# Opening shared PSUM banks by the first product, storing pairs of tiles from two queues, and delaying the first squares in a decoder trunk

## The chip, the cores and the metric

The kernel runs on one core of a Trainium2 chip. The time is the device time of one execution in microseconds (us); before the change it is 1935.7 us, the median of three runs (1936.59, 1935.7, 1930.64). The engines are called as in the profile: PE (TensorE) with PEld for its weight loads, DVE (VectorE), ACT (ScalarE), POOL (GpSimd) and SP (SyncE, which here only issues DMAs).

## The reference, cut to what matters

A trunk of two layers works on 512 tokens and 16 meta tokens with a model width of 1024. Each layer is FFN, mixer, FFN; each of these has an RMS norm in front and one behind it, and is added to the residual stream `h`:

```python
def rmsnorm(x, g):
    return x * lax.rsqrt(jnp.mean(x * x, axis=-1, keepdims=True) + EPS) * g

def swiglu(x, w_in, w_out):
    gate, up = jnp.split(x @ w_in, 2, axis=-1)
    return (jax.nn.silu(gate) * up) @ w_out
```

Layer 0 mixes by chunked gated linear attention. Behind it one set of keys and values is made from `h`. Layer 1 mixes by sliding-window attention over that set. All is float32, the hidden width of the FFNs is 2816, and the 512 ordinary tokens of the last `h` are the output.

## The kernel before, in words

**Layout.** The residual stream `H` lies in SBUF as 128 partitions x 8 k tiles x 528 tokens, the features on the partitions. Layer 0 works on two groups of tokens, 272 and 256 (`L0`), layer 1 on two of 256 (`L1`). In the names of tiles, l0f is a first or second FFN of layer 0, l0m its mixer, kv the shared keys and values, l1f and l1m those of layer 1.

**A product** x @ w is made of three matmuls in fp32r (`mm3s`, L333): weight and operand are each split into a high and a low part, and high x high, low x high and high x low are added in one PSUM bank. The weights come by DMA as raw tiles of 128 x 512; `split_part` (L224) copies the high part on ACT (L226) and subtracts it on DVE (L227). The operand of an FFN or mixer is split in the same way by `Operand.build` (L425 on ACT, L426 on DVE).

**The norm** in front isn't applied to the operand but to the result, so the products needn't wait for it. `Operand.sumsq` squares the eight k tiles of `H`; squares 0 and 7 are kept (L399, ACT), 1 to 6 are squared on ACT (L402) and added on POOL (L403). `rstd` (L348) adds them over the partitions by products with ones (st_...), makes the reciprocal root in ten small operations on DVE or POOL (av, yv, zv, wv), puts it on a diagonal (dg, L383) and spreads it by a product (r_...). `Operand.factors` (L436) copies the result on ACT (R_..., L442). The gates need it: `gu` (L617), silu (L618), the up half (L621, L622) and the split of the hidden layer (`hid`, L407 and L408).

**The opening of an FFN or mixer** is `x_first` (L509): the first four units (128 output features each) of group 0, then of group 1, each over the eight k tiles, with the results kept in PSUM until the factor is there. A group of at most 256 tokens shares a bank between two units ("shared", L528): each has a half of 256 columns. As the products of the two units alternate, a product of 128 x 512 with a matrix of zeros opens each bank (L532, two per group), and the products add to it.

**The order of the work** is written out by a recorder, `Flow` (L60): jobs are generators with due times on a clock that each recorded product advances by its estimated time (L161 to L167). `flow.pump()`, called in `mm3s`, runs the jobs that are due. The order in which the jobs are run, with the waits that their data ask for, is the order in the queues of the engines. `spawn(job, delay)` sets when a job starts.

**The start of the kernel** (L1195 to L1244) loads the first k tiles of `H` and the first weights, builds group 0 (L1231 to L1235), spawns its squares, sum and factor (`factors(0)`, L1205, with a delay of 2.0; L1236) and group 1's operand (`second`, L1212, with a delay of 6.0; group 1's squares come when it is built). A square is due every 0.4 of the clock.

**The end** is `Residual.store` (L471): for each group and each pair of k tiles DVE multiplies the last FFN's result by its factor (L479), DVE or POOL (for the first two pairs of the last group) adds it to `H` (L480), and SP stores the two tiles, 128 KB each, by two DMAs (L482).

Of the kernel before, what the change touches and what calls it, by code (L numbers as in the profile page):

```python
# [16 lines left out]
P = 128  # L17
D = 1024
KD = 8
META = 16  # L20
# [103 lines left out]
def trunk_kernel(ctx: ExitStack, tc, a, out):  # L124
    nc = tc.nc
    pe, act, dve, pool, sp = nc.tensor, nc.scalar, nc.vector, nc.gpsimd, nc.sync
    flow = Flow()
# [7 lines left out]
    H = cp.tile([P, KD, TOK], F32, name="H")  # L135
# [6 lines left out]
    zeros = cp.tile([P, P], F32R, name="zeros")  # L142

    def ps(name):
        return pp.tile([P, 512], F32, tag="ps", name=name)

    def pair_tile(name, dt=F32R):
        return hp.tile([P, 2, TOK], dt, tag="pair", name=name)
# [5 lines left out]
    def flat(t):  # L154
        return t.rearrange("p a t -> p (a t)")

    def gain(layer, i, k):
        c = V_GAIN + layer * 48 + i * 8 + k
        return vec[:, c : c + 1]

    def mm(o, lhs, rhs, start=True, stop=True, onto=False):  # L161
        inst = pe.matmul(o, lhs, rhs, start=start, stop=stop, skip_group_check=onto)  # L162
        n = 1
        for d in rhs.shape[1:]:
            n *= d
        flow.clock += n / 2400 if rhs.dtype == F32R else max(n / 600, 0.12)
        return inst  # L167
# [41 lines left out]
    def set_ahead(n, slots=None):  # L209
        ahead[0], limit[0] = n, slots or n  # L210
        room[0].finish(flow)
        room[0] = Job(None)
# [11 lines left out]
    def split_part(i, raw, m):  # L224
        w = pair_tile(f"w{i}_{len(loaded[i])}")
        act.activation(w[:, 0, :m], raw[:, :m], AF.Copy)  # L226
        dve.tensor_tensor(w[:, 1, :m], raw[:, :m], w[:, 0, :m].bitcast(F32), op=ALU.subtract)  # L227
        loaded[i].append(w)
# [71 lines left out]
    def prefetch():  # L300
        while len(loaded) < cap[0] and asked[0] + costs[len(loaded)] <= freed[0] + ahead[0]:
            if isinstance(units[len(loaded)], list) and chains[0] == CHAINS:
                break
            load_unit()

    def next_w():
        used[0] += 1
        prefetch()
        flow.until(lambda: len(loaded) >= used[0])
        flow.wait(split_jobs[used[0] - 1])  # L310
        return loaded[used[0] - 1]
# [16 lines left out]
    def done_w(n=1):  # L328
        free_slots(sum(costs[released[0] : released[0] + n]))
        released[0] += n  # L330


    def mm3s(outs, j, x, g, start, stop, shared=False):  # L333
        t, n = g
        cols = slice(j % 4 * P, (j % 4 + 1) * P)
        xh, xl = x[:, 0, t : t + n], x[:, 1, t : t + n]
        for o, w in outs:
            mm(o, w[j // 4][:, 0, cols], xh, start and not shared, False)
            mm(o, w[j // 4][:, 1, cols], xh, False, False)
        for i, (o, w) in enumerate(outs):  # L340
            mm(o, w[j // 4][:, 0, cols], xl, False, stop and (not shared or i % 2 == 1))
            flow.pump()

    def mm3(o, w, j, x, g, start, stop):
        mm3s([(o, w)], j, x, g, start, stop)
# [64 lines left out]
    class Operand:  # L410
# [25 lines left out]
        def factors(self, gi, eng=pool):  # L436
            if self.rt is None:
                self.rt = sm.tile([P, TOK], F32, tag="R", name=f"R_{self.name}", bufs=2)
            o, n = self.groups[gi]
            yield FACT  # L440
            r = yield from rstd(self.accs[gi], n, D, False, f"{self.name}_{o}", eng)
            act.activation(self.rt[:, o : o + n], r[:, :n], AF.Copy)  # L442
# [5 lines left out]
    class Residual:  # L448
# [22 lines left out]
        def store(self, gi, g, r):  # L471
            o, n = g
            rb = r[:, :n].unsqueeze(1).to_broadcast([P, 2, n])
            for k in range(0, KD, 2):
                h, y = H[:, k : k + 2, o : o + n], Y[:, k : k + 2, o : o + n]
                last = gi == 1 and k < 4
                t = flat(pair_tile(f"t_{self.name}{k}", F32))[:, :512] if last else ps(f"t_{self.name}{gi}{k}")
                t = t.rearrange("p (k n) -> p k n", n=n)
                dve.tensor_tensor(t, y, rb, op=ALU.mult)  # L479
                (pool if last else dve).tensor_tensor(h, t, h, op=ALU.add)  # L480
                for j in (k, k + 1):
                    sp.dma_start(out[j, :, o - META : o - META + n], H[:, j, o : o + n])  # L482
                yield 1.0


# [23 lines left out]
    def x_first(x, nu, evac, opening=False, behind=(), first_ahead=8):  # L509
        behind = list(behind)  # L510
        ws = [] if opening else [next_w() for _ in range(nu)]
        set_ahead(8 if opening else 2 * first_ahead)
        jobs = []

        def drain(gi, g, some, pst):
            yield x.rjob[gi]
            for i, p in zip(some, pst):
                evac(i, g, p)
                yield 0.6

        both = range(nu)
        order = [(0, both[: nu // 2]), (0, both[nu // 2 :])] if opening else [(0, both)]
        for gi, some in order + [(1, both)]:
            g = x.groups[gi]
            n = g[1]
            while len(ws) <= some[-1]:
                ws.append(next_w())
            shared = n <= 256  # L528
            if shared:
                banks = [ps(f"x{used[0]}_{i}_{gi}") for i in some[::2]]  # L530
                for b in banks:
                    mm(b.rearrange("p (a c) -> p a c", c=P), zeros, zeros.unsqueeze(1).to_broadcast([P, 4, P]), True, False)  # L532
                pst = [banks[i // 2][:, i % 2 * 256 : i % 2 * 256 + n] for i in range(len(some))]
            else:
                pst = [ps(f"x{used[0]}_{i}_{gi}")[:, :n] for i in some]
            for k in range(KD):
                x.need(gi, k)
                mm3s([(p, ws[i]) for i, p in zip(some, pst)], k, x.tiles[k], g, k == 0, k == KD - 1, shared)
            flow.until(lambda: x.rjob[gi] is not None)
            jobs.append(flow.spawn(drain(gi, g, some, pst)))  # L540
            if gi == 0 and some[-1] == nu - 1:
                cap[0] = len(units)
                prefetch()
            if behind:
                flow.spawn(behind.pop(0))
        done_w(nu)
        return jobs
# [56 lines left out]
    def ffn(x, groups, finish, opening=False, tail=4):  # L604
# [31 lines left out]
        for ci, (lo, hi) in enumerate(FF_CHUNKS):  # L636
            hids = []
            if ci == 0:
                jobs = x_first(x, 4, evac_to([new_hid() for _ in range(2)]), opening)
                set_ahead(16, 4)  # L640
                factors = flow.spawn(right_factors(x, halves, z, plain))
                for t in range(2, hi):
                    jobs += x_units(x, 2, groups, evac_to([new_hid()]))
                plain.finish(flow)
                set_ahead(16, 8)
            else:
                flow.wait(factors)
                set_ahead(16, RING)
                tiles = Strassen(z, halves)
                cur = tiles.head(new_hid())  # L650
                while cur:
                    tiles.body(cur)
                    nxt = tiles.head(new_hid()) if len(hids) < hi - lo else None
                    jobs.append(tiles.tail(cur, nxt is None))
                    cur = nxt
            flow.wait(*jobs)
            if lo < LAST:
                out_proj(hids, groups, x.groups, ci == 0)
            else:
                set_ahead(32)  # L660
                cap[0] = min(used[0] + NLAST + tail, len(units))
                out_proj(hids, groups, x.groups, False, finish, KD, True)
# [119 lines left out]
    def gla(x, finish):  # L782
        set_ahead(10)
        with tc.tile_pool(name="gp", bufs=1) as gp:
# [193 lines left out]

            kinds = [("lr", 0), ("k", 0), ("q", 0), ("v", 0)]
            drained = x_first(x, 4, lambda i, g, p: evac(*kinds[i], g, p), first_ahead=5)  # L980
            flow.spawn(resets())
            gate = flow.spawn(gates(drained))
# [23 lines left out]
    def shared_kv(x, kp, behind):  # L1006
# [21 lines left out]
        def place(drained):  # L1028
# [3 lines left out]
            for j in range(2):  # L1032
# [21 lines left out]
                yield 1.0  # L1054

        job = flow.spawn(place(x_first(x, 4, evac, behind=behind, first_ahead=6)))
        return (kz, vt, vmz), job

# [139 lines left out]
    x = Operand("l0f0", lambda k: gain(0, 0, k), L0)  # L1198
# [32 lines left out]
    for c in (0, 512):  # L1231
        for k in range(c // 128, c // 128 + 4):
            x.build(0, k)
            if k % 4 < 2:
                split_part(k % 4, raws[k % 4][c // 512], 512)  # L1235
    x.rjob[0] = flow.spawn(factors(0), 2.0)  # L1236
    dma_end[0] = 1.0
    load_unit()
    load_unit()
# [13 lines left out]
    x = nxt  # L1253
    nxt, fin = into("l0f1", 0, 3, False, lambda k: gain(0, 4, k), L0)
    gla(x, fin)
    x = nxt
# [4 lines left out]
    with tc.tile_pool(name="kp", bufs=1) as kp:  # L1261
        x = Operand("l1f0", lambda k: gain(1, 0, k), L1)
# [10 lines left out]
        x = nxt  # L1273
# [88 lines left out]
```

## Time and profile before

| what | us |
|---|---|
| median of three runs | 1935.7 |
| the runs | 1936.59, 1935.7, 1930.64 |
| the profiled execution | 1931.38 |
| its span, first to last instruction | 1929.5 |
| PE busy | 1888.9 (98%) |
| DVE busy | 1420.1 (74%) |
| ACT busy | 1001.7 (52%) |
| POOL busy | 215.1 (11%) |
| mean granted clock of PE | 0.996 |

The profile is that of one execution, the one in the table. In a row of the timeline the columns are the start and the length in us, the engine, the line of the kernel, the operation, output <- inputs by the program's names (without their numbers), shapes and the count of the instructions joined; in brackets stands how long the engine was idle before, and what ended that. The lines are those of the kernel before; in the changed one they are higher by three from L333 on, and by one from L532 on. In a row of windows come the busy time of PE, PEld, DVE, ACT and POOL with their instructions, the granted clock, the share of the DMA engines and GB/s.

### The profile page before, as it was taken

Reading aid. Unit: us, or ns where it says so; the run is one execution under the profiler, and the core shown is the slowest. Engines: PE = TensorE matmul, PEld = TensorE weight load, DVE = VectorE, ACT = ScalarE, POOL = GpSimd, SP = SyncE. Lnnn points to the kernel's source line nnn. Section 1 sums busy time; section 2 is a strip of 40 time slices with the busy share of each in tenths; the row PEclk is TensorE's granted clock in tenths of the full one; section 3 lists DMA queues with packets and bytes.
Section 4 is the critical chain, followed back from the end, with each engine's and each line's share of the span. In section 5 each row is a group of like instructions: output and inputs, shape, how many; then the busy total and the mean of one; then the engine's idle time right before and its main releaser. Section 6 shows DMA issues by size and latency. Waiting matters only on the chain.

```text
span 1929.5 us, 37402 instructions
## 1 busy us (share of the span) xinstructions
PE 1888.9 (98%) x14522; PEld 1798.1 (93%) x14522; DVE 1420.1 (74%) x2868; ACT 1001.7 (52%) x2268; POOL 215.1 (11%) x417
## 2 busy tenths in 40 slices
PE   8999999999999999999999999999998999999997
PEld 7999999999999999999999898989976898989897
DVE  7885858676464788585887786868788779858584
ACT  5663636653245555353574453535645665636363
POOL 2000000321111400000033000000352140000002
PEclk9999999999999999999999999999999999999998
DMA  4332333322113123323351123233421212333331
GB/s 163 104 100 88 103 96 106 114 74 69 45 52 113 56 72 95 102 91 102 99 176 45 61 88 115 87 112 99 132 66 34 77 45 72 98 105 107 101 112 44
DMA packets 102144, 174.61 MB, mean 90 GB/s; under 512 B 11472, under 2 KB 24272, under 8 KB 101968
## 3 DMA queue, kind: packets, MB, share of 16 engines
q1 hardware_dynamic: 101680, 172.11, 28.2%
q8 instruction: 113, 1.85, 0.4%
q14 instruction: 63, 0.52, 0.1%
q10 hardware_dynamic: 288, 0.13, 0.0%
HBM read 170.10 MB, written 2.10 MB: 89 GB/s over the span
## 4 chain that ended last, share of the span: by engine, by line
PE 70%; DVE 19%; ACT 6%; issue 3%; POOL 1%; DMA 0%; SPq 0%; DVEq 0%; ACTq 0%; POOLq 0%
PE y L162 30%; PE x L162 16%; PE a L162 11%; DVE raw L251 5%; PE c L162 4%; DVE w_s L246 3%; DVE w L246 3%; ACT w_s L245 3%; PE d L162 2%; DVE w L227 2%; PE o L162 1%; ACT w L226 1%; PE po L162 1%; DVE hidl0f L775 1%; PE sc L162 0%
## 5 line engine op out<-in xcount | busy, mean ns | idle before, releaser
L246 DVE TENSOR_TENSOR w_s<-raw,w_s 128x512 fp32r<-128x512 f32 x288 | 194.0, 690 | 129.7 <-ACT w_s L245 127.6
L227 DVE TENSOR_TENSOR w<-raw,w 128x512 fp32r<-128x512 f32 x378 | 244.9, 673 | 31.1 <-ACT w L226 29.3
L162 PE MATMUL y<-hidl0f,w 128*128 128x256 f32 (+1 forms) x2112 | 261.0, 285 | 0.0
L162 PEld LDWEIGHTS y<-hidl0f,w 128*128 128x128 f32 x2112 | 258.8, 188 | 0.7
L245 ACT ACTIVATE w_s<-raw 128x512 fp32r<-128x512 f32 x288 | 175.3, 628 | 149.5 <-DVE raw L251 146.0
L162 PE MATMUL y<-hidl1f,w 128*128 128x512 f32 (+1 forms) x1344 | 249.8, 346 | 0.0
L162 PEld LDWEIGHTS y<-hidl1f,w 128*128 128x128 f32 x1344 | 212.0, 188 | 33.9 <-ACT hidl1f L774 0.4
L226 ACT ACTIVATE w<-raw 128x512 fp32r<-128x512 f32 x378 | 209.0, 586 | 46.0 <-PE y L162 39.4
L403 POOL TENSOR_TENSOR acc_post<-acc_post,sq_post 128x256 f32<-128x256 f32 (+1 forms) x72 | 56.9, 791 | 1386.5 <-ACT sq_post L402 1386.0
L251 DVE TENSOR_TENSOR raw<-raw,raw 128x512 f32<-128x512 f32 x288 | 198.0, 687 | 5.5
L246 DVE TENSOR_TENSOR w<-raw,w 128x512 fp32r<-128x512 f32 x216 | 148.3, 687 | 41.5 <-ACT w L245 40.2
L245 ACT ACTIVATE w<-raw 128x512 fp32r<-128x512 f32 x216 | 133.9, 621 | 48.0 <-PE y L162 47.7
L162 PE MATMUL x<-x_l0m,w 128*128 128x272 f32 (+1 forms) x1200 | 158.3, 288 | 0.0
L162 PEld LDWEIGHTS x<-x_l0m,w 128*128 128x128 f32 x1200 | 149.4, 189 | 1.2
L572 DVE TENSOR_TENSOR Y<-y,Y 128x256 f32<-128x256 f32 (+2 forms) x176 | 83.0, 473 | 74.4 <-PE y L162 73.8
L162 PE MATMUL a<-zl0f_t,w_s 128*128 128x264 f32 x864 | 117.8, 285 | 3.8 <-ACT c L751 3.8
L162 PE MATMUL a<-zl1f_t,w_s 128*128 128x256 f32 x864 | 115.1, 282 | 2.0 <-ACT c L751 1.6
L162 PEld LDWEIGHTS a<-zl0f_t,w_s 128*128 128x128 f32 x864 | 110.1, 188 | 5.0 <-ACT c L751 5.0
L162 PEld LDWEIGHTS a<-zl1f_t,w_s 128*128 128x128 f32 x864 | 106.9, 188 | 4.8 <-ACT c L751 4.8
L162 PE MATMUL x<-x_l0f,w 128*128 128x256 f32 (+1 forms) x768 | 100.0, 290 | 7.5 <-ACT w L226 5.8
L162 PEld LDWEIGHTS x<-x_l0f,w 128*128 128x128 f32 x768 | 96.6, 191 | 8.9 <-ACT w L226 5.8
L162 PE MATMUL x<-x_l1f,w 128*128 128x256 f32 (+1 forms) x576 | 93.1, 320 | 0.0
(485 smaller groups left out, 3306.5 us busy)
## 6 DMA issues: line engine op xcount, KB each, us to landing
raw<-in_w_in SPq DMA_DIRECT2D x352, 256.0 KB, 2.9
raw<-in_w_out SPq DMA_DIRECT2D x96, 256.0 KB, 3.3
raw<-in_gla_in SPq DMA_DIRECT2D x50, 256.0 KB, 3.0
raw<-in_w_last SPq DMA_DIRECT2D x48, 256.0 KB, 3.1
raw<-in_w_out SPq DMA_DIRECT2D x64, 128.0 KB, 3.0
raw<-in_gla_out SPq DMA_DIRECT2D x16, 256.0 KB, 2.9
raw<-in_w_q SPq DMA_DIRECT2D x16, 256.0 KB, 3.6
raw<-in_swa_out SPq DMA_DIRECT2D x16, 256.0 KB, 2.8
```

The lines of the kernel that those rows point to most:

```text
L162: inst = pe.matmul(o, lhs, rhs, start=start, stop=stop, skip_group_check=onto)
L226: act.activation(w[:, 0, :m], raw[:, :m], AF.Copy)
L227: dve.tensor_tensor(w[:, 1, :m], raw[:, :m], w[:, 0, :m].bitcast(F32), op=ALU.subtract)
L245: act.activation(w[:, 0, :512], src, AF.Copy)
L246: dve.tensor_tensor(w[:, 1, :512], src, w[:, 0, :512].bitcast(F32), op=ALU.subtract)
L251: dve.tensor_tensor(dst, dst, src, op=ALU.add)
L403: pool.tensor_tensor(sums[0][:, :n], sums[0][:, :n], t[:, :n], op=ALU.add)
L572: dve.tensor_tensor(y, p[:, :n], y, op=ALU.add)
L775: dve.scalar_tensor_tensor(t.hid[:, 1, g], t.h, -1.0, t.hid[:, 0, g].bitcast(F32), op0=ALU.mult, op1=ALU.subtract)
```

## The change

Three things are changed. In `mm3s` the first product of the first unit of a shared bank opens the bank (start), and the second unit's products are all written as adding to an opened bank; `x_first` issues no zero products any more. In `store` each pair of k tiles goes out in one DMA of 256 KB, and in the last group the second and fourth pair are issued by ACT's queue instead of SP's. In the start of the kernel the delay of `factors(0)` is 9.0 instead of 2.0.

```diff
     def mm3s(outs, j, x, g, start, stop, shared=False):
...
-        for o, w in outs:
-            mm(o, w[j // 4][:, 0, cols], xh, start and not shared, False)
-            mm(o, w[j // 4][:, 1, cols], xh, False, False)
         for i, (o, w) in enumerate(outs):
-            mm(o, w[j // 4][:, 0, cols], xl, False, stop and (not shared or i % 2 == 1))
+            second = shared and i % 2 == 1
+            mm(o, w[j // 4][:, 0, cols], xh, start and not second, False, second)
+            mm(o, w[j // 4][:, 1, cols], xh, False, False, second)
+        for i, (o, w) in enumerate(outs):
+            second = shared and i % 2 == 1
+            mm(o, w[j // 4][:, 0, cols], xl, False, stop, second)
             flow.pump()
...
-                for j in (k, k + 1):
-                    sp.dma_start(out[j, :, o - META : o - META + n], H[:, j, o : o + n])
+                to = out[k : k + 2, :, o - META : o - META + n].rearrange("k p n -> p k n")
+                (act if gi and k % 4 else sp).dma_start(to, h)
...
                 banks = [ps(f"x{used[0]}_{i}_{gi}") for i in some[::2]]
-                for b in banks:
-                    mm(b.rearrange("p (a c) -> p a c", c=P), zeros, zeros.unsqueeze(1).to_broadcast([P, 4, P]), True, False)
...
-    x.rjob[0] = flow.spawn(factors(0), 2.0)
+    x.rjob[0] = flow.spawn(factors(0), 9.0)
```

In the order of the engines' queues this takes the twenty zero products from PE and changes no other product; it replaces sixteen DMAs by six on SP and two on ACT. At the start of the kernel, squares 5 to 7 of group 0 come on ACT behind the copy of the third and fourth weight unit and behind the operand of group 1; st_l0f of group 0 comes on PE behind seven of the eight k tiles of group 1 (before: ahead of them); r_l0f of group 0 is followed on PE by the fifth unit's products, whose weights ACT copies behind R_l0f, the table load, two silu and two hid. Elsewhere some operations of ACT, DVE and POOL trade places by a few instructions: in layer 1's mixer POOL's addition of square 6 comes behind two operations of the rotary embedding (L1002, L1003).

## The prediction

> **What bounds the kernel now.** I read the page first (shares, then the chain), then what TensorE waited for, then the stretches around each edit.
>
> ```profile
> span 1929.5 us, 37402 instructions
> PE 1888.9 (98%) x14522; PEld 1798.1 (93%) x14522; DVE 1420.1 (74%) x2868; ACT 1001.7 (52%) x2268; POOL 215.1 (11%) x417
> PE 70%; DVE 19%; ACT 6%; issue 3%; POOL 1%; DMA 0%; SPq 0%; DVEq 0%; ACTq 0%; POOLq 0%
> ```
>
> TensorE is busy 98% of the span, so a product taken off its queue is worth its step there, unless a wait that other engines end stands behind it and swallows the gain. The second view lists these waits:
>
> ```profile
> PE x L162 <- ACT w L226: 5.8, 1, 5.8
> ...
> PE x L162 <- DVE w L227: 1.7, 3, 0.9
> ...
> PE st_l1m L162 <- POOL acc_l1m L403: 1.1, 1, 1.1
> PE st_l0f L162 <- ACT acc_l0f L399: 1.1, 1, 1.1
> ...
> PE st_kv L162 <- POOL acc_kv L403: 0.7, 1, 0.7
> ...
> PE r_l0f L162 <- DVE dg_l0f L383: 0.6, 1, 0.6
> ```
>
> Columns: total us, times, longest. Three of them (st_l1m, st_l0f, st_kv) come a few us behind zero products; the 5.8, the 1.7 and the 0.6 lie in the opening, which the third edit rearranges.
>
> **Edit 1: the zero products.**
>
> ```profile
> L162 PE MATMUL x<-zeros x20: 388/396/402, 23.3 to 1572.9; 128*128 128x512 f32 x20
> 23.32 0.64 PE L162 MATMUL x<-zeros 128*128 128x512 f32 x2
> 23.80 1.46 PE L162 MATMUL x<-x_l0f,w 128*128 128x256 f32 x11
> ```
>
> Twenty, in ten pairs. From the first of a pair to the next ordinary product are 23.80 - 23.32 = 0.48 us; that, and not the 0.39 that each lasts, is what a pair holds of the queue. Gross 10 x 0.47 = 4.7 us. No instruction takes their place: the first half's first product opens the bank. Pair by pair: one lies in the opening (below). Layer 0's mixer (one pair) and the second pair of layer 1's first FFN have no wait of the list behind them: -0.47 each. In layer 0's second FFN (one pair, st_l0f), at the shared keys and the FFN that follows them (two pairs, st_kv) and in layer 1's mixer (two pairs, st_l1m) the next sum waits for squares whose chain begins at a factor product queued ahead of the zeros; the zeros only fill that wait. I take +0.1 for the first (a moved weight split), 0 for the second and 0 for the third; each has bounds of -0.5 and +0.5, the third a rival of its own. The two pairs of layer 1's second FFN have no wait behind them either, but a factor chain whose product comes hardly later than its dg: I take -0.6 of their 0.94. Sum without the opening: -0.47 - 0.47 + 0.1 - 0.6 = **-1.4** (bounds -3.2 and 0).
>
> **Edit 3: first squares later.** This is the part that I worked through row by row, with the changed kernel's queue order laid beside the old one's rows.
>
> ```profile
> 13.60 0.74 ACT L402 ACTIVATE sq_l0f<-H 128x272 f32<-128x272 f32 x2
> 14.06 3.64 DVE L227 TENSOR_TENSOR w<-raw,w 128x512 fp32r<-128x512 f32 x4
> ...
> 14.57 1.14 ACT L226 ACTIVATE w<-raw 128x512 fp32r<-128x512 f32 x2
> ...
> 17.16 3.66 PE L162 MATMUL x<-x_l0f,w 128*128 128x272 f32 x27 [0.90 <-DVE w L227]
> ...
> 20.65 1.09 PE L162 MATMUL st_l0f<-ones,acc_l0f 128*68 128x1 f32 x16
> ...
> 25.81 0.73 PE L162 MATMUL r_l0f<-dg_l0f,ones 68*128 68x272 f32 x2 [0.56 <-DVE dg_l0f L383]
> ...
> 26.18 10.43 PE L162 MATMUL x<-x_l0f,w 128*128 128x256 f32 x85
> 26.58 0.40 ACT L442 ACTIVATE R_l0f<-r_l0f 128x272 f32<-128x272 f32 x1 [2.88 <-PE r_l0f L162]
> ...
> 29.92 2.18 ACT L226 ACTIVATE w<-raw 128x512 fp32r<-128x512 f32 x4
> ...
> 36.44 0.95 PE L162 MATMUL st_l0f<-ones,acc_l0f 128*128 128x1 f32 x8
> ...
> 37.25 2.55 PE L162 MATMUL x<-x_l0f,w 128*128 128x272 f32 x19
> 37.43 0.16 DVE L361 TENSOR_SCALAR av_l0f<-st_l0f 128x2 f32<-128x2 f32 x1 [4.36 <-PE st_l0f L162]
> ...
> 39.40 0.42 DVE L383 TENSOR_TENSOR dg_l0f<-ident,yv_l0f 128x256 f32<-128x256 f32 x1
> ```
>
> Gain: ACT's squares at 13.60 go behind the fourth unit's weight copy (14.57), which then runs up to 1 us earlier; the wait of 0.90 shrinks to about 0.4 (-0.5).
>
> Loss: the sum st_l0f of group 0 (20.65) now stands behind seven of the eight k tiles of group 1. Group 1's 96 products take 11 (23.80) and 85 (26.18), without the factor's wait and step 36.44 - 23.80 - 0.56 - 0.37 = 11.7 us, 0.122 each. They now begin at 23.80 - 0.5 - 0.96 (the sum at 20.65, 1.09 with its drain, is moved away) - 0.48 = 21.9. Seven k tiles, 84 products: 32.1; the sum: 33.1; the last 12: 34.5; st_l0f of group 1: 35.35, as the queue's step (its last results come near 35.5). VectorE's ten small operations on group 0's sum take 0.2 us each (37.43 to 39.40), but now an operation on group 1's sum is queued among them, so the last ones start at 35.5 and dg is done at about 36.55. TensorE idles from 35.35 to 36.6: **1.2 us**. The next product needs the weight copy w4 on ACT, and there R, the table load, two silu and two hid stand ahead of it, as before: its first of four (2.18 in all) ends at about 30.54, 30.54 - 25.81 = 4.73 after r's start, so now at 36.6 + 4.75 = 41.4. TensorE's step for r ends at 37.0, so it idles **4.4 us**. Before, this delay was covered by the 85 products; now only r, with nothing else, stands in front of it.
>
> What stood behind 37.25 starts at 41.4: +4.1. Counted by waits it is the same: 0.4 + 1.2 + 4.4 = 6.0 against 0.90 + 0.56 = 1.46, less the zeros' 0.48, is +4.1. VectorE does not stop this from being carried on:
>
> ```profile
> 42.00:61.40 19.40, 19.40 (x162) 19.40 (x161) 19.40 (x40) 9.72 (x21) 0.00 (x0) 1.00 0.23 68
> ```
>
> ```profile
> 41.04 0.42 DVE L617 TENSOR_TENSOR gu<-x,R_l0f 128x256 f32<-128x256 f32 x1 [1.21 <-ACT R_l0f L442]
> ...
> 61.44 13.84 PE L162 MATMUL y<-hidl0f,w 128*128 128x272 f32 x112
> ```
>
> The window's columns are us, then the busy time of PE, PEld, DVE, ACT and POOL, the clock, the DMA share and GB/s. VectorE is full beside TensorE there, but the work that began at 41.04 now begins behind the four weight splits that follow w4, at about 41.5 + 4 x 0.6 = 43.9, +2.9, less than TensorE's 4.1, so it isn't the later of the two. If it were, y (61.44) would show it. Nor can TensorE, full too, win anything back.
>
> A second cost comes from the granted clock:
>
> ```profile
> 6.72 3.28 PE L162 MATMUL x<-x_l0f,w 128*128 128x272 f32 x13 [0.28 <-DVE w L227]
> ...
> 1454.00:1457.00 3.00, 1.94 (x8) 1.08 (x8) 2.97 (x8) 2.38 (x10) 1.04 (x1) 1.00 0.00 0
> 1457.00:1460.00 3.00, 2.71 (x13) 1.71 (x15) 3.00 (x11) 0.67 (x3) 0.00 (x0) 0.51 0.57 180
> 1460.00:1461.00 1.00, 1.00 (x17) 1.00 (x16) 1.00 (x4) 0.09 (x1) 0.00 (x0) 0.75 0.00 0
> ```
>
> Behind a gappy stretch of attention the clock (the column ahead of the DMA share) was halved for some 3.5 us; and the first 13 products of the kernel took 3.28 us, 0.25 each, against 3.66 for 27, 0.136 each, later. A gap of 4.4 us with one of 1.2 before it should halve it again. At half rate for 3.5 us half the work is done: 1.6 us lost (bounds 0 and 3). Opening: 4.1 + 1.6 = **+5.7** (bounds: +2.5, the gap shorter by what ACT could do earlier and no halving, and +7.5, the halving over 7 us).
>
> The Trainium skill, "TensorE: Matmul & The Clock Gate", in "Part 1: The HAM clock gate (the "warmup" mystery)", says that about 3.4 us without work halve the clock, and about 3.4 us of work restore it. The 0.51 agrees in size; by that rule the loss would be near 1.7.
>
> **Edit 2: the stores.**
>
> ```profile
> 1921.85 2.49 POOL L480 TENSOR_TENSOR H<-t_out,H 128x512 f32<-128x512 f32 x2 [6.79 <-DVE t_out L479]
> 1923.14 4.00 SPq L482 DMA_DIRECT2D out<-H x8
> 1923.48 1.28 DVE L480 TENSOR_TENSOR H<-t_out,H 128x512 f32<-128x512 f32 x2
> ...
> 1926.00:1927.00 1.00, 0.00 (x0) 0.00 (x0) 0.00 (x0) 0.00 (x0) 0.00 (x0) 0.50 0.83 278
> ...
> out<-H SPq DMA_DIRECT2D x8, 128.0 KB, 1.8
> ```
>
> Now the eight issues fill SP's queue until 1927.14, 0.5 each, 2.4 us past VectorE's last sum (1924.76); the last begins near 1926.65 and lands 1.8 later, at 1928.45. Changed, two are issued on SP and two on ACT, which has nothing left to do: the first pair at 1923.14 as before, the others behind their sums at about 1924.2, 1924.35 (POOL's end, 1924.34) and 1924.8. Then the transfers bind. At 278 / 0.83 = 335 GB/s a store of 128 KB takes 0.4 of its 1.8 us, so 1.4 are fixed; three pairs, 786 KB, take 2.35. From 1924.2 that is 1924.2 + 1.4 + 2.35 = 1927.95, 0.5 earlier; by the last issue alone it would be 1.85 earlier. I take **-0.6**, near the first, since the queues are full (bounds -1.85 and 0).
>
> The Trainium skill, "DMA: Bandwidth & Descriptors", in "Issuing engines are not separate DMA queues", says that a second issuing engine adds no bandwidth and saves only issue time. By that the gain ends where the transfers bind, as in the sum; no run here shows two queues.
>
> **Sum.** -1.4 + 5.7 - 0.6 = **+3.7 us**. The profiled execution took 1931.38 us (span 1929.5 and 1.9 around it), which gives 1935.1. It is one of the faster ones: the runs lie at 1930.64, 1935.7 and 1936.59. On the median of the runs, 1935.7, the forecast is **1939.4**, +0.19%; the times below are on that median too.
>
> **Rivals.**
> *The stall without the halved clock.* For: in 1454 to 1457 TensorE was busy for 1.94 us of 3.00 and the clock was still whole, and here r's products cut the idle time in two. Against: 4.4 us at one go. +3.7 - 1.6 = +2.1: 1937.8.
> *The opening is hidden*, if group 0's chain ends so early that w4 is copied ahead of need, and the zeros' time isn't swallowed: 4.7 for the zeros, 0.6 for the stores, 0.5 for the squares: -5.8, 1929.9; with the waits of the list swallowing theirs, -3.0. For: TensorE is the bound, and each product gone counts. Against: r can't start before a sum that stands behind seven k tiles.
> *Slower, by the attention stage*:
>
> ```profile
> 1416.12 2.04 POOL L403 TENSOR_TENSOR acc_l1m<-acc_l1m,sq_l1m 128x256 f32<-128x256 f32 x2
> 1418.12 0.73 POOL L1002 TENSOR_TENSOR sh_q<-sh_q,csq 128x256 f32<-128x256 f32 x1
> 1418.93 0.74 POOL L1003 TENSOR_TENSOR q<-q,sh_q 128x256 f32<-128x256 f32 x1
> ```
>
> The changed order puts POOL's last addition behind those two. If they are not ready earlier, st_l1m waits 1.5 us longer than its 1.1, and with TensorE 0.9 earlier the gap passes 3 us, where the clock may fall: 1.5 + 1.6 on top of 3.7 = +6.8: 1942.5. It decides when that addition ends after about 1419. For the other side: ACT's and VectorE's weight splits go behind the squares there, so these should be ready earlier.
> *The zeros are not what holds the queue* (the first product into a bank takes their time): +1.4 on the forecast, 1940.8, inside its range.
>
> **How the numbers follow.** The forecast with its own range (1937 to 1941) 0.45, which holds the last rival too; without the halved clock 0.15; hidden 0.12; attention 0.28. About 0.3%, 5.8 us, is what this kernel's runs can tell from no change. Faster by more: two thirds of the hidden case, 0.08; slower by more: 0.28; within: 0.64. The range takes in the hidden case's 1930 and the attention case's 1942.5 with the opening's upper bound, 1.8 above: 1930 to 1944.
>
> **What would show it.** No "x<-zeros" group; a wait of r_l0f near 35 us of over 1 us and one of "x <- ACT w" of some 4 us at 37; the clock at 0.5 somewhere in 39 to 46; y's first product near 67 instead of 61.44; the stores' last issue some 2 us before its old place, as seen from VectorE's last sum. The forecast is wrong if w4 is copied ahead of R on ACT, or if the sum of group 0 is taken earlier than after seven k tiles.

## The result, and the profile after

The changed kernel takes **1944.07 us** (median of six runs, 1942.25 to 1946.6) against 1934.95 for the one before (six runs): a ratio of **1.0045**, 95% interval 1.0035 to 1.0055, some 8.7 us slower (the two medians lie 9.1 apart). The forecast was +3.7, 1939.4, with "within 0.3%" at 0.64. The direction came as forecast and the size did not: the result lies at the upper end of the range of 1930 to 1944, and it is the case "slower by more", to which 0.28 was given. The profiled execution is the longest of the six (1946.6), so part of its distance to the profile before (1931.38, near the shortest) is spread between runs; why runs spread is seen below.

The page of the changed kernel, span and engines:

```profile
span 1944.8 us, 37347 instructions
PE 1898.5 (98%) x14502; PEld 1807.1 (93%) x14502; DVE 1416.1 (73%) x2868; ACT 1002.2 (52%) x2268; POOL 215.9 (11%) x417
```

TensorE has exactly twenty instructions less and is busy 9.6 us longer. The windows below show that products of the same shape took longer where the granted clock was halved. What TensorE waited for (total us, times, longest):

```profile
PE x L162 <- ACT w L226: 10.3, 3, 6.0
...
PE st_l1m L162 <- POOL acc_l1m L406: 3.1, 1, 3.1
...
PE st_kv L162 <- POOL acc_kv L406: 1.1, 1, 1.1
...
PE r_kv L162 <- POOL dg_kv L386: 1.0, 1, 1.0
PE r_l0f L162 <- DVE zv_l0f L369: 0.9, 1, 0.9
...
PE r_l1f L162 <- POOL dg_l1f L386: 0.8, 1, 0.8
...
PE x L162 <- DVE w L227: 0.3, 1, 0.3
```

Against the list before, the wait for weights has grown by 4.5 us, st_l1m by 2.0, r_kv by 0.8, r_l1f by 0.8 (it was not listed) and st_kv by 0.4; the waits for DVE's splits have shrunk by 1.4. At r_kv and st_kv, 1.2 us together, it is time of the zero products that now passes in waiting. At r_l1f it is not: no zero product stood between its sum and it.

**The opening** in the timeline, PE and ACT:

```profile
34.09 0.95 PE L162 MATMUL st_l0f<-ones,acc_l0f 128*128 128x1 f32 x8
35.92 0.70 PE L162 MATMUL r_l0f<-dg_l0f,ones 68*128 68x272 f32 x2 [0.89 <-DVE zv_l0f L369]
40.72 0.81 PE L162 MATMUL x<-x_l0f,w 128*128 128x272 f32 x2 [4.09 <-ACT w L226]
...
66.86 1.40 PE L162 MATMUL y<-hidl0f,w 128*128 128x272 f32 x10
```

```profile
36.66 0.40 ACT L445 ACTIVATE R_l0f<-r_l0f 128x272 f32<-128x272 f32 x1 [12.24 <-PE r_l0f L162]
37.07 1.28 ACT L619 ACT_TABLE_LOAD   x1
38.37 0.75 ACT L619 ACTIVATE gu<-gu 128x272 f32<-128x272 f32 x2
39.36 0.78 ACT L410 ACTIVATE hidl0f<-gu 128x272 fp32r<-128x272 f32 x2 [0.24 <-DVE gu L623]
40.05 2.17 ACT L226 ACTIVATE w<-raw 128x512 fp32r<-128x512 f32 x4
```

ACT goes with one pause of 0.24 from R to the weight copy, and TensorE waits 4.09 us for that. y begins at 66.86 instead of 61.44, 5.4 later. In the windows (the granted clock is the column after POOL's count) the clock falls to half during the wait and stays there behind it:

```profile
36.00:39.00 3.00, 0.62 (x2) 0.19 (x2) 2.77 (x13) 2.31 (x4) 0.00 (x0) 0.98 0.02 5
39.00:42.00 3.00, 1.28 (x5) 1.20 (x5) 2.78 (x7) 2.76 (x7) 0.00 (x0) 0.50 0.00 0
42.00:45.00 3.00, 3.00 (x14) 2.91 (x14) 3.00 (x6) 1.03 (x3) 0.00 (x0) 0.50 0.70 197
45.00:48.00 3.00, 3.00 (x24) 3.00 (x23) 3.00 (x8) 0.75 (x2) 0.00 (x0) 0.88 0.42 152
```

From 42 to 45 TensorE is full with 14 products, where before, at the whole clock, it did 162 in 19.4 us, some 25 in three.

**Layer 1's mixer.** POOL's additions, TensorE's sum, and the windows:

```profile
1421.29 1.17 POOL L406 TENSOR_TENSOR acc_l1m<-acc_l1m,sq_l1m 128x256 f32<-128x256 f32 x1
1422.42 0.91 POOL L1003 TENSOR_TENSOR sh_q<-sh_q,csq 128x256 f32<-128x256 f32 x1
1423.40 1.05 POOL L1004 TENSOR_TENSOR q<-q,sh_q 128x256 f32<-128x256 f32 x1
1424.42 0.72 POOL L406 TENSOR_TENSOR acc_l1m<-acc_l1m,sq_l1m 128x256 f32<-128x256 f32 x1
```

```profile
1425.19 0.59 PE L162 MATMUL st_l1m<-ones,acc_l1m 128*128 128x1 f32 x2 [3.09 <-POOL acc_l1m L406]
```

```profile
1421.00:1424.00 3.00, 1.10 (x10) 0.89 (x8) 3.00 (x5) 0.61 (x2) 2.92 (x4) 1.00 0.27 81
1424.00:1427.00 3.00, 1.81 (x8) 1.81 (x9) 0.84 (x2) 0.81 (x2) 1.14 (x2) 0.62 0.36 94
1427.00:1430.00 3.00, 3.00 (x17) 3.00 (x15) 0.00 (x0) 0.00 (x0) 0.00 (x0) 0.50 0.00 0
1430.00:1433.00 3.00, 3.00 (x13) 2.85 (x13) 0.45 (x2) 0.26 (x1) 1.82 (x10) 0.50 0.00 0
1433.00:1436.00 3.00, 3.00 (x10) 2.36 (x9) 0.00 (x0) 0.00 (x0) 0.94 (x3) 0.68 0.00 0
```

The two operations of the rotary embedding stand between the last two additions and hold the sum up by 0.91 + 1.05; behind it the clock is halved for 10.2 us, though TensorE is full. Instruction by instruction the changed kernel is 5.0 us behind the old one at the second group's first product (1413.46 against 1408.46) and 11.4 us behind after this stretch.

**The end**, SP and ACT queue, DVE, and the stores' landing:

```profile
1939.07 1.42 SPq L485 DMA_DIRECT2D out<-H  x2
1939.41 1.28 DVE L483 TENSOR_TENSOR H<-t_out,H 128x512 f32<-128x512 f32 x2
1940.30 0.94 ACTq L485 DMA_DIRECT2D out<-H  x2
```

```profile
out<-H SPq DMA_DIRECT2D x2, 256.0 KB, 2.1
out<-H ACTq DMA_DIRECT2D x2, 256.0 KB, 2.9
```

From VectorE's last sum (1940.69) to the end (1944.8) are 4.1 us; before they were 1929.5 - 1924.76 = 4.7.

### The profile page after: what moved, and what is told of

Same layout as the page of the kernel before. It is cut to its first block, busy times and chain, and to the rows that moved or that the text cites. A ratio compares the mean times of both kernels' runs of the same rounds, so it can differ in the third digit from the quotient of the medians.

```text
span 1944.8 us, 37347 instructions
## 1 busy us (share of the span) xinstructions
PE 1898.5 (98%) x14502; PEld 1807.1 (93%) x14502; DVE 1416.1 (73%) x2868; ACT 1002.2 (52%) x2268; POOL 215.9 (11%) x417
## 4 chain that ended last, share of the span: by engine, by line
PE 71%; DVE 18%; ACT 6%; issue 3%; POOL 1%; DMA 0%; SPq 0%; DVEq 0%; ACTq 0%; POOLq 0%
PE y L162 30%; PE x L162 17%; PE a L162 11%; DVE raw L251 5%; PE c L162 4%; DVE w_s L246 3%; DVE w L246 3%; ACT w_s L245 3%; PE d L162 2%; PE o L162 1%; DVE w L227 1%; PE sc L162 1%; ACT w L226 1%; PE po L162 1%; DVE hidl0f L776 1%
```

## The experiments

Theory: the opening costs idle time and a halved clock, layer 1's mixer the same through POOL's order, and the zeros' time is mostly swallowed by waits. Rivals: all of it is the opening; or the clock falls by chance; or the removed products never held TensorE up. Each kernel was timed in five rounds against the kernel before. Their intervals are 0.0009 to 0.0012 to either side, some 2 us, so smaller differences are not read from the times.

**delay_only**: before, with the third edit alone.

```diff
-    x.rjob[0] = flow.spawn(factors(0), 2.0)
+    x.rjob[0] = flow.spawn(factors(0), 9.0)
```

> Only the delay of factors(0) is 9.0, the zero products and the eight stores stay. Theory (the opening as forecast): r_l0f waits about 0.9 us and the fifth unit about 4 us for its weight copy near 37 us, the clock is halved for some 6 us behind that, y begins near 67.3 instead of 61.44: +5.9 us (4.5 to 7), a ratio near 1.003, and the order behind the opening is that of before. Rival (the opening's loss is an accident of the queue order that only the removed zeros cause): y within 1 us of 61.44, no change.

1941.33 us, ratio **1.0032** (1.0020 to 1.0045). The waits are 0.9 and 4.09 us, y begins at 67.06, 5.6 us late, and behind the opening the list of the waits is that of before. The opening as forecast is confirmed, and it needs no missing zeros.

**after_delay2**: the changed kernel with the third edit undone.

```diff
-    x.rjob[0] = flow.spawn(factors(0), 9.0)
+    x.rjob[0] = flow.spawn(factors(0), 2.0)
```

> The changed kernel with the delay back at 2.0: zeros gone, stores by pairs. Theory (the loss outside the opening comes from the reordered mixer of layer 1): st_l1m still waits about 3 us for POOL's addition, the clock is halved behind it, and the sum is +1 to +5 us. Rival (all of the loss is the opening): the zeros and the stores bring 3 to 5 us, st_l1m waits below 2 us, 1930 to 1932 on a median of 1935.

1936.79 us, **1.0010** (1.0001 to 1.0019): the first two edits, which take work away, make the kernel no faster. With 1.0032 for the third it is the whole of the 1.0045, within the intervals. TensorE in layer 1's mixer, and the windows:

```profile
1418.12 0.38 PE L162 MATMUL st_l1m<-ones,acc_l1m 128*128 128x1 f32 x2 [3.10 <-POOL acc_l1m L406]
```

```profile
1418.00:1421.00 3.00, 2.88 (x17) 2.88 (x18) 0.35 (x1) 0.00 (x0) 0.07 (x1) 0.67 0.23 80
1421.00:1424.00 3.00, 3.00 (x16) 3.00 (x16) 0.00 (x0) 0.26 (x1) 0.97 (x5) 0.50 0.00 0
```

The same wait of 3.1 and the halved clock. The rival "all is the opening" falls. Compared instruction by instruction with the trace of before, this one leads by 1.1 us as it comes to the mixer's two pairs of zeros, by 2.1 after them (each pair gave 0.47) and by 0.1 at the sum, and it trails by 3.0 from 1427 on. So the sum comes 1.0 later, with the zeros' 0.94 already gained, and after it another 3.1 are lost.

**zeros_kept_order**: zeros gone, but the recorder's clock advanced as before, so POOL's and SP's order stays that of before (ACT's and DVE's but for a few neighbours).

```diff
-                for b in banks:
-                    mm(b.rearrange("p (a c) -> p a c", c=P), zeros, zeros.unsqueeze(1).to_broadcast([P, 4, P]), True, False)
+                flow.clock += len(banks) * 512 / 2400
```

(with `mm3s` as in the change)

> Before, with the zero products gone but the recorder's clock advanced as if they were there, so that POOL's and SP's order is that of before and ACT's and DVE's all but so. Theory (the order, not the missing products, makes st_l1m wait): no wait of 3 us, st_l1m waits 1.1 to 2.0 us as TensorE comes up to 0.9 us earlier; gain 2 to 3 us. Rival (TensorE's earlier arrival is enough to halve the clock there): st_l1m waits 2 us, the clock falls behind it, and the gain is eaten: -1 to +4 us.

1935.49 us, **0.9997** (0.9988 to 1.0006). The wait did what the theory said:

```profile
PE st_l1m L162 <- POOL acc_l1m L405: 1.6, 1, 1.6
```

but the time did not: a gain of 2 to 3 us was expected, and the interval runs from -2.3 to +1.2. In its profile st_kv (1.1) and r_kv (1.2) wait 1.4 longer than before, what three pairs of zeros are worth, and the clock is halved from 1437.7 on for 6.8 us where it was whole in the profile before. The 0.8 of r_l1f is not in its list, so that wait comes from the order. This run alone does not decide what the zeros are worth.

**store_only**: before, with the stores of the change.

```diff
-                for j in (k, k + 1):
-                    sp.dma_start(out[j, :, o - META : o - META + n], H[:, j, o : o + n])
+                to = out[k : k + 2, :, o - META : o - META + n].rearrange("k p n -> p k n")
+                (act if gi and k % 4 else sp).dma_start(to, h)
```

> Before with the paired stores from two queues alone. Theory (transfers bind): the span from the last addition to the end is 0.4 to 0.8 us shorter; in the time no more than -0.05%. Rival (issues bind): 1.8 us shorter. Second rival: the larger stores land later, no gain.

1934.21 us, 0.9996 (0.9987 to 1.0005); in the trace from the last sum (1929.72) to the end (1933.8) 4.1 us, 0.65 less than before. "Transfers bind" holds. Up to its end this kernel is that of before, so its trace is a second one of the same program, and it shows why runs differ. Windows of this trace, then the same of before:

```profile
572.00:575.00 3.00, 3.00 (x16) 3.00 (x16) 2.70 (x8) 1.98 (x6) 0.00 (x0) 0.55 0.03 5
...
668.00:671.00 3.00, 3.00 (x19) 3.00 (x18) 0.43 (x1) 0.00 (x0) 2.25 (x10) 0.62 0.95 271
```

```profile
572.00:575.00 3.00, 3.00 (x27) 3.00 (x26) 2.77 (x7) 1.18 (x4) 0.00 (x0) 1.00 0.02 5
...
668.00:671.00 3.00, 2.81 (x22) 2.61 (x21) 0.00 (x0) 0.00 (x0) 1.99 (x8) 1.00 0.84 266
```

Behind the same waits (r_go 1.6, st_l0f 1.1) the clock fell in one run and not in the other. The profile on which the prediction rests had one halved stretch of 3.4 us before the last norm; this one has 3.4 at 571, 3.4 at 667, 6.8 at 1459 and 3.4 at 1489.

**delay_fill**: delay_only, and sixteen products of zeros ahead of the fifth unit, in the bank that its first product opens anew; they add work to TensorE and change no value.

```diff
+            if not filled:
+                filled.append(i)
+                fill(pst[0], 16)
             for k in range(KD):
...
+    def fill(bank, m):
+        for _ in range(m):
+            pe.matmul(bank.rearrange("p (a c) -> p a c", c=P), zeros, zeros.unsqueeze(1).to_broadcast([P, 4, P]), start=True, stop=True)
```

> Delay 9.0 alone, and between r_l0f and the first product that waits for w4 sixteen products of zeros (16 x 0.23 = 3.7 us), which write a bank that the next product opens anew. Theory (the opening costs idle time and, apart from it, a halved clock): the fifth unit still starts near 41 us, the clock stays whole from 36 to 47, and of delay_only's 6.1 us about 1.6 to 2.0 are gone: +4.3 us, a ratio near 1.0022. Rival (the clock doesn't go by TensorE's own work, or zeros don't count as work): halved as in delay_only, 1.0032.

1940.35 us, **1.0024** (1.0015 to 1.0033). PE, and the windows:

```profile
36.39 4.01 PE L337 MATMUL x<-zeros 128*128 128x512 f32 x16
40.85 0.52 PE L162 MATMUL x<-x_l0f,w 128*128 128x272 f32 x2 [0.45 <-ACT w L226]
...
64.76 3.46 PE L162 MATMUL y<-hidl0f,w 128*128 128x272 f32 x27
```

```profile
39.00:42.00 3.00, 2.55 (x14) 1.79 (x13) 2.78 (x7) 2.76 (x7) 0.00 (x0) 1.00 0.00 0
42.00:45.00 3.00, 3.00 (x27) 3.00 (x26) 3.00 (x7) 1.15 (x3) 0.00 (x0) 1.00 0.64 201
```

The real products begin as late as in delay_only (40.85, 40.82), the clock is whole, and y begins at 64.76, 3.3 us behind before, where delay_only's (67.06) is 5.6 behind; up to 566 us the two stay 3.6 and 6.0 behind. So the opening is 3.3 of waiting and 2.3 of clock. (The 3.3 hangs on the profile of before; in store_only, which has the same opening, y begins at 60.66, 0.8 earlier.) The times agree (1.0024 and 1.0032) but would not tell it alone.

**delay2_fill**: after_delay2, and twelve products of zeros ahead of st_l1m in its own bank (the fourteen products of the group that stand inside the sum in after_delay2 then follow it).

```diff
         st = ps(f"st_{name}")
+        if name == "l1m_272":
+            fill(st, 12)
```

> The changed kernel with delay 2.0 and twelve products of zeros (2.8 us) ahead of the sum st_l1m that waits 3.1 us for POOL in layer 1's mixer. Theory (that wait halves the clock, for 6.9 us after it): no halved clock from 1416 to 1427, 3 us less than after_delay2: about 1933.5, ratio 0.999. Rival (the clock would have fallen there anyway, or zeros don't count): as after_delay2, 1.001.

1933.53 us, **0.9988** (0.9979 to 0.9997), 0.0022 below after_delay2. TensorE, and the windows:

```profile
1413.84 2.90 PE L336 MATMUL st_l1m<-zeros 128*128 128x512 f32 x12
1417.17 1.05 PE L162 MATMUL st_l1m<-ones,acc_l1m 128*128 128x1 f32 x8 [0.42 <-POOL acc_l1m L412]
```

```profile
1418.00:1421.00 3.00, 3.00 (x26) 3.00 (x27) 0.03 (x2) 0.26 (x1) 1.73 (x9) 1.00 0.01 2
1421.00:1424.00 3.00, 3.00 (x15) 2.45 (x14) 0.41 (x1) 0.00 (x0) 1.03 (x4) 1.00 0.00 0
```

The sum comes no earlier for it (from 3.1 us ahead of before, TensorE falls back to 1.0 ahead at the sum, by 2.0 as in after_delay2), POOL's order is the same, and apart from the fourteen products only the clock differs: whole, and behind the sum nothing more is lost, where after_delay2 lost 3.1. So the wait itself halves the clock, and most of what layer 1's mixer costs is the clock.

**after_kept**: the changed kernel with the recorder's clock kept (the line shown at zeros_kept_order); it differs from it only in the order.

> The changed kernel with the recorder's clock kept, so that POOL's order in layer 1's mixer is that of before; only this differs. Theory (the changed kernel's loss beyond the opening is that order): st_l1m waits 1.6 instead of 3.1 us, 1.0045 falls to delay_only's 1.0032 less the gains, about 1.0025. Rival (its loss is in the opening and by chance in the clock): 1.0040 or more.

1940.47 us, **1.0025** (1.0015 to 1.0036), 0.0020 or 3.9 us below the change. st_l1m waits 1.6 us again. The order is what the removed products cost. Its trace still has the clock halved for 6.8 us behind that wait, so 1.6 us can be enough.

**best**: zeros gone with the clock kept, stores by pairs, delay 2.0.

> Zero products gone with the recorder's clock kept, paired stores, delay 2.0: the parts of the change that should pay. Theory: the store's 0.65 us and, of the 4.7 us of zeros, the 2 that no wait takes: -1 to -2.7 us, ratio 0.9986 to 0.9995. Rival (the zeros' time is lost to further halvings in attention, as zeros_kept_order's 0.9997 may say): the store alone, 0.9996.

1934.71 us, 0.9995 (0.9986 to 1.0004); the clock was halved from 1419.6 on in its trace too. Between the theory and its rival it decides nothing.

**after_fill**: the changed kernel with all three fills, 16 in the opening, 6 ahead of the last r_go (`if name == "go3_0": fill(r, 6)`), 12 ahead of st_l1m.

> The changed kernel whole, with products of zeros in three waits: sixteen ahead of the fifth unit in the opening, six ahead of the last r_go in layer 0's mixer, twelve ahead of st_l1m in layer 1's. Theory (its loss is idle time in the opening plus halved clock there and in layer 1's mixer): 1.0045 less 1.7 us in the opening, 3.3 in layer 1's mixer and 0.5 at r_go is 1.0016, a bit under 1939. Rival (waits alone cost): 1.0035 or more.

1937.16 us, **1.0007** (0.9998 to 1.0016). 34 products more, and 0.0038 or 7.3 us faster than the changed kernel: more than the 5.5 that were expected. What remains of the loss, 1.4 us, should be the opening's 3.3 of waiting, less what the first two edits bring.

**before_fill**: before with fills alone, 6 ahead of the last r_go, 4 ahead of st_l1m.

> The kernel before with six products of zeros ahead of the last r_go (wait 1.6 us) and four ahead of st_l1m (wait 1.1), nothing else. Theory (its runs differ by the number of halved stretches, and one of them comes at r_go in most runs): 0.5 to 1.5 us less, 0.9993 to 0.9997. Rival (those waits are too short to matter): 1.0000.

1935.8 us, 0.9999 (0.9990 to 1.0008): the rival. In its trace the clock is whole behind r_go, but no gain is seen in the times; the fills are worth nothing here that can be measured.

**best_fill**: best with 6 and 6.

> Zero products gone with the recorder's clock kept, paired stores, delay 2.0, and six products of zeros each ahead of the last r_go and of st_l1m. Theory (the zeros' gain was eaten by halvings at these two waits): 0.9995 falls by 1.5 to 3 us, to 0.9980 to 0.9988. Rival (it never was there): 0.9995.

1933.05 us, **0.9986** (0.9977 to 0.9995). Against before_fill, which has fills at the same places, it is 2.7 us faster. The order is held, but not the clock: the granted clock of its runs is 0.994 to 0.995, that of before_fill's 0.993 to 0.994, and of the 2.1 us that its trace is ahead at 1900, 1.2 were won at 667, where before_fill's clock fell behind st_l0f and its own did not. That leaves some 0.9 of the zeros' 4.7, by the traces, and 0.65 by the stores; the times do not part them. It is the fastest version with the next, and beats both kernels.

**delay2_fill2**: delay2_fill with 6 ahead of the last r_go.

> Zero products gone in the order of the changed kernel, paired stores, delay 2.0, twelve products of zeros ahead of st_l1m and six ahead of the last r_go. Theory: 0.9988 of the run without those at r_go falls by some 0.5 to 1 us, to 0.9984; best_fill should beat it by the shorter wait in layer 1's mixer, 1.5 us less, which the intervals may not part. Rival: the r_go wait is no place where the clock falls, 0.9988.

1933.53 us, 0.9986 (0.9977 to 0.9995), as delay2_fill (0.9988): r_go is no place that can be measured, and the longer wait in layer 1's mixer, once filled, isn't seen beside best_fill. Neither part of the expectation can be seen.

## Why the prediction was right, and where its size was off

*The opening, +5.7.* Right in its mechanism, step by step. The waits were 0.89 and 4.09 (forecast 1.2 and 4.4), y began at 66.86 (near 67), delay_only measured 0.0032, 6.2 us. That the sum fits so well is in part luck, for two of its terms were off against each other. The halved clock cost about 2.3 us by the traces of delay_only and delay_fill, not 1.6: it lasted for 6.8 us, not 3.5, of which the first 1.7 passed while TensorE waited anyway. That leaves 3.1 of the 5.4 us for the waiting, not 4.1; the earlier waits for splits shrank by 1.4 (1.7 to 0.3), not by 0.5. One of the two rows that spoke for it doesn't show it: where the first 13 products took 3.28 us, the granted clock in the profile is 1.00.

*The stores, -0.6.* Right: -0.65 in the trace.

*The zeros.* The gross step of 0.47 a pair held, against the rival that the zeros are not what holds the queue: in after_delay2's trace TensorE goes from 1.1 to 1.6 us ahead of before across the pair at 1394. Where I said that waits swallow it, at the shared keys, they did (st_kv +0.4, r_kv +0.8). The step "-0.6 of their 0.94" for layer 1's second FFN failed: the two pairs gave their 0.9, but r_l1f, without a listed wait before, now waits 0.8 us for POOL's dg. The zeros did not cause that wait, for they stand ahead of the sum on which the chain hangs. From the sum's first product to the end of dg the chain took 6.7 us before (1583.46 to 1590.12), and 7.4 in the changed kernel (1598.37 to 1605.75), because single operations on POOL took longer there; first before, then changed:

```profile
1585.60 0.32 POOL L367 TENSOR_TENSOR zv_l1f<-zv_l1f,av_l1f 128x2 f32<-128x2 f32 x1
```

```profile
1600.51 0.71 POOL L370 TENSOR_TENSOR zv_l1f<-zv_l1f,av_l1f 128x2 f32<-128x2 f32 x1
...
1605.81 0.70 PE L162 MATMUL r_l1f<-dg_l1f,ones 128*128 128x256 f32 x2 [0.81 <-POOL dg_l1f L386]
```

With the zeros gone and the order kept (zeros_kept_order, after_kept, best) the wait is not in the list. So it comes with the order; why the operations took longer in it is not shown.

*Layer 1's mixer, taken as 0.* This is the term that made the result: the rival "slower, by the attention stage", at 0.28, is what happened, by its own mechanism (the last addition behind the two rotary operations; it ended at 1425.14, with TensorE waiting since 1422.10). I had its wait at 1.1 + 1.5 plus TensorE's earlier arrival and measured 3.1. "For the other side" I had argued that the squares would be ready earlier because the weight splits go behind them; they were, but POOL stood in the rotary operations first. The order of the queue was on the table and would have carried it. Its price in the sum is +1.0, not the 2.0 by which the wait grew: the zeros' 0.94 there was already taken as swallowed. The rival had 1.5.

*Its clock, 1.6.* Too small: two or three times 3.4 us instead of one, 3.1 us behind the sum in after_delay2's trace and 4.4 in the changed kernel's. The times of after_delay2 and delay2_fill differ by 0.0022, 4.3 us, by this and by the products that trade places with the sum.

*The base.* The sum was made against one profiled execution, which with one halved stretch was near the fastest of its kernel. That such stretches come and go between runs at r_go, st_l0f and in attention was not in the forecast; it blurs every number here by a multiple of some 1.7 us.

With +1.0 for the later sum, 3.1 for its clock, and 0 for layer 1's second FFN, the sum is 3.7 + 1.0 + 3.1 + 0.6 = +8.4; measured are +8.7, and what the base blurs is more than the difference.

## What to carry to other kernels

Where one engine is busy 98% of the time, a removed instruction pays only if nothing behind it waits on a chain that starts ahead of it; look for the next wait, not at the share. An order that a recorder's clock decides is moved by every product taken out or put in: compare the queues of the side engines, and price each operation that now stands ahead of one that the bound engine waits for. A wait of 3 us on TensorE cost more than its length here, because the clock fell; products of zeros in the wait, into a bank that is opened anew, avoided that. In shorter waits (before_fill) they brought nothing that could be measured. Before two times are compared, compare the granted clock of their runs.

## What the runs showed of the hardware

Halved stretches of the granted clock came in whole steps: in all fourteen traces they lasted 3.4, 6.8 or 10.2 us, none between (apart from the last one, which runs into the end of the trace), and went on at full work (10.2 us from 1424.7 on in the changed kernel, with TensorE full for 9.7 of them). In each trace they also start on one grid: in the changed kernel at 38.89, 670.36, 1424.70, 1448.60, 1469.08 and 1499.80, which are 0, 185, 406, 413, 419 and 428 steps of 3.413 us from the first. Where the grid lies differs from run to run. The Trainium skill, "TensorE: Matmul & The Clock Gate", "Part 1: The HAM clock gate (the "warmup" mystery)", has windows of about 3.4 us that run free; the steps agree. That one window of full work restores the clock, as it also says, was so in the opening and in the stretches of 3.4 us; in layer 1's mixer it took two (after_delay2, TensorE full from 1418.1, whole again at 1425.8) or three (the changed kernel).

A whole window without work was not needed: waits of 3.1 us (after_delay2) and 1.6 us (after_kept) were followed by a halved clock, and the same waits of 1.6 and 1.1 us in two runs of one program (r_go, st_l0f) once were and once weren't. The grid tells the first of these two apart: the wait at r_go fell into one step in store_only (567.9 to 571.3, TensorE busy for 0.51 of it, halved behind it), and in before onto the border of two (at 569.6; busy for 0.72 and 0.79, not halved). Over all fourteen traces, from 20 us up to the last stretch, a step at the whole clock in which TensorE was busy for less than half was always followed by a halved one, and one with more than three quarters never; between them both happened, so that the share alone does not decide. Products of zeros keep the clock whole as others do (delay_fill, delay2_fill).
